# A decoder block on one core: the seventh product of a unit is put behind the next unit's first two

## The chip, the core and the metric

The kernel runs on one core of one Trainium2 chip. Five engines work side by side, each on its own queue in order: TensorE (PE in the profile; its weight loads are PEld), VectorE (DVE), ScalarE (ACT), GpSimd (POOL) and SyncE (SP), which here issues all DMA transfers. The metric is device time in microseconds, the median of the runs shown.

## The reference

One decoder layer over 2048 positions of width 1024, in float32. The input is normalised (RMSNorm) and projected once; the columns feed two mixers side by side. Their outputs are joined, projected, and added to the input; then comes a SwiGLU FFN of inner width 2816 with a residual, and a last RMSNorm.

```python
h = rmsnorm(x, norm1_g[l])
proj = h @ w_in[l]
p_q, p_k, p_v, p_g, p_a, c_b, c_c, c_h = jnp.split(proj, splits, axis=-1)
...
o = gla_chunked(q, k, v, log_a)          # 4 heads, 64 keys, 128 values, chunks of 64
o = rmsnorm(o, gla_norm_g[l]) * jax.nn.silu(p_g)
u = c_c * c_h
o_conv = c_b * causal_depthwise_conv(u, conv_w[l])   # width 3
mixed = jnp.concatenate([o_gla, o_conv], axis=-1) @ w_out[l]
x = x + mixed
h2 = rmsnorm(x, norm2_g[l])
ffn = (jax.nn.silu(h2 @ w_ffn_gate[l]) * (h2 @ w_ffn_up[l])) @ w_ffn_down[l]
x = x + ffn
return rmsnorm(x, norm_f_g)
```

## The kernel before

**Units of seven products.** The activations lie transposed, in blocks of 512 positions; the kernel works through them in two halves of two blocks each. The large products are done as 2 by 2 blocks: a unit (`unit`, L452) makes a 2 by 2 result, quarters (r, j) with r a block of 128 columns of the weights and j one of the half's two position blocks, by seven products instead of eight, in Strassen's manner (Winograd's form). `PRODUCTS` (L36) names the seven pairs of a weight quarter or a combination of quarters (A11, S1, S2, A12, S3, S4, A22) and an operand (B11, T1, T2, B21, T3, B22, T4). `unit_weights` (L424) loads the four quarters as one block `raw` (two buffers), makes S1 to S4 on POOL in place (S1 in a tile `s1` of its own) and splits each of the seven into a high and a low part (`split`, L162: one ACT instruction, then one DVE instruction), into tiles `wq` with four buffers. `product_step` (L443) adds high by high, high by low and low by high: three matmuls of 128 x 512 for each of the n blocks of 128 rows. n is 4 in the mixer's input projection and in FFN up, so a product has 12 matmuls; in the FFN's down projection it is 2 for the first group of inner blocks and 3 for the three others, 6 and 9 matmuls.

**Banks.** The eight PSUM banks come from one pool. A unit takes three: `oa` for the first, third, fifth and seventh product, `ob` for the second and sixth, and a third one for the fourth. Between two products in one bank the first has to be taken out: `copied` (ACT copy at L480, or, where the result is added to a running sum, `plus` on DVE at L473), and `plus` after the fourth, fifth and sixth product. The seventh is left in its bank, and whoever called `unit` takes it from there (`settled`, `silu`) or has it copied.

```python
oa = mul(0)
c11 = copied("c11", oa, (0, 0))
ob = mul(1)
c22 = copied("c22", ob, (1, 1))
mul(2, oa)
c12 = copied("c12", oa, (0, 1))
plus(c11, mul(3))
mul(4, oa)
plus(c22, oa)
mul(5, ob)
plus(c12, ob)
mul(6, oa)
```

**Stages.** `in_proj` (L749) runs twelve units for each half: keys and queries, values, the output gate, and for the convolution two rounds of three factors. Behind every second product `tick` (L241) takes one step of background work, among it the linear attention (`gla_half`), which `in_proj` starts after its sixth unit. Then `out_proj` (L935) without Strassen; for each half `ffn_up` (L1048), eleven pairs of a gate and an up unit, whose results go to DRAM split (`split_later`), and `ffn_down` (L1083), four groups of inner blocks (`GROUPS`) with four units each that add into tiles `y`. The last unit of all, `last_unit`, uses plain products with the final norm between them. The operands of a half or a group are loaded by `load_pairs`, `load_h2` or `group_op` into 28 tiles `op`; some (`WHOLE`) come unsplit and are split behind their load.

**Order.** The kernel is recorded in program order, and a scheduler of the tile layer then orders the instructions of each engine by its own model of time, so that a product's matmuls can stand interleaved with those of others. Marks (`issue_after`, `behind`) hold single instructions behind others.

Of the kernel before, what the change touches and what calls it, by code (L numbers as in the profile page):

```python
# [10 lines left out]
F32 = mybir.dt.float32  # L11
# [26 lines left out]
    ("S3", "T3"), ("S4", "B22"), ("A22", "T4"),  # L38
# [3 lines left out]
LATER = ("B21", "T3", "B22", "T4")  # L42
# [10 lines left out]
def tile_hymba_block(ctx, tc, x, xt, win, wa, wgu, wout, wffn, wdown, wdown_first, small, out):  # L53
# [370 lines left out]
    def unit_weights(src, raw=None):  # L424
# [7 lines left out]
        pool.tensor_tensor(a11, s1, a11, ALU.subtract)  # L432
# [4 lines left out]
        pool.tensor_tensor(a12, a12, a11, ALU.subtract)  # L437
# [14 lines left out]
    def unit(src, ops, into=None, onto=None, raw=None):  # L452
# [3 lines left out]
        w = unit_weights(src, raw)  # L456
# [25 lines left out]


# [178 lines left out]
    def load_pairs(src):  # L662
        ops = no_operands()
        for _, n in PRODUCTS:
            ops[n] = [(load_whole if n in WHOLE else load_pair)(p) for p in src[n]]
        return ops

# [81 lines left out]
    def in_proj(half, ops, first=None, differences=None):  # L749
        def units():  # L750
            for u in range(12):
                with ExitStack() as stack:
                    if half == 0 and u == 1:
                        stack.enter_context(tc.issue_after(last_load[0].ins))
                    if half or u > 1:
                        us = unit(win[u], ops)
                    else:
                        us = plain_unit(win[u], ops, differences) if u else first
                if half == 0 and u == 1:
                    del ops["B12"]  # L760
                    differences(("T4",))
                yield us

        units = units()
        for dst, i0 in ((s_kq, 0), (s_kq, 2), (s_v, 0), (s_v, 2)):
            for r, j, c, p in next(units):
                store(dst[2 * half + j][i0 + r][:], settled(c, p)[:])
        for i0 in (0, 2):
            for r, j, c, p in next(units):
                store(s_g[2 * half + j][i0 + r][:], silu(c, p)[:])  # L770
        background.append(gla_half(half))
        for i0 in (0, 2):
            cc = {(r, j): settled(c, p) for r, j, c, p in next(units)}
            ch = {(r, j): c for r, j, c, _ in next(units)}
            for r in range(2):
                i = i0 + r
                left = halo[:, i, :]
                for j in range(2):
                    s = tp.tile([P, PB + 2], F32, name="u", tag="t")
                    dve.tensor_tensor(s[:, 2:], ch[r, j][:], cc[r, j][:], ALU.mult)  # L780
                    act.activation(s[:, 0:2], left, AF.Copy)
                    left = s[:, PB : PB + 2]
                    y = cc[r, j]
                    act.activation(y[:], s[:, 0:PB], AF.Copy, scale=col(C_CW + i))
                    for n in (1, 2):
                        dve.scalar_tensor_tensor(
                            y[:], s[:, n : n + PB], col(C_CW + 4 * n + i), y[:], ALU.mult, ALU.add
                        )
                if half == 0:
                    act.activation(halo[:, i, :], left, AF.Copy)  # L790
            for r, j, c, _ in next(units):
# [7 lines left out]


# [238 lines left out]
    def load_h2():  # L1039
        ops, loads = no_operands(), raw_loads[-2]  # L1040
        for _, n in PRODUCTS:
            for k in range(4):
                with tc.issue_after(loads.ins):
                    o = (load_whole if n in WHOLE else load_pair)(s_h2p[n][k])
                ops[n].append(o)
        return ops

    def ffn_up(half, ops):  # L1048
        for m in range(NF // 2):
            us = unit(wffn[2 * m], ops)  # L1050
            sg = {(r, j): silu(c, p) for r, j, c, p in us}
            for r, j, c, _ in unit(wffn[2 * m + 1], ops):
                s = sg[r, j]
                dve.tensor_tensor(s[:], c[:], s[:], ALU.mult)
            b11, b12, b21, b22 = [sg[r, j] for r in range(2) for j in range(2)]
            t1, t2, t3, t4 = [bt(n) for n in ("t1", "t2", "t3", "t4")]
            for y, p, q in ((t1, b12, b11), (t2, b22, t1), (t3, b22, b12), (t4, b21, t2)):
                pool.tensor_tensor(y[:], p[:], q[:], ALU.subtract)
            values = [("B11", b11), ("B21", b21), ("B22", b22)]
            if half == 1 and m >= LAST_GROUP:  # L1060
                values.append(("B12", b12))
            values += [("T1", t1), ("T2", t2), ("T3", t3), ("T4", t4)]
            background.insert(0, split_later(s_act[half][m], values))
# [18 lines left out]

    def ffn_down(half):  # L1083
# [6 lines left out]
        for u, m0 in enumerate(GROUPS):  # L1090
# [4 lines left out]
            raw = None  # L1095
            if u:
                raw = raw_weights(wdown[4 * u - 4])
                with tc.issue_after(raw_loads[-1].ins):
                    ops = {n: [group_op(m, n) for m in ms] for _, n in PRODUCTS}
            else:  # L1100
                ops = {n: [group_op(m, n) for m in ms] for _, n in PRODUCTS}
# [5 lines left out]
            for d0 in range(0, KD, 2):  # L1107
# [6 lines left out]
                if u == 0:  # L1114
# [5 lines left out]
                    unit(src, ops, {(r, j): y[d0 + r, j] for r in range(2) for j in range(2)})  # L1120
                    continue
                xs = []
                if u < 3:
                    for d in (d0, d0 + 1):
                        xs.append((y[d, u - 1], bt("x1")))
                        load(xs[-1][1][:], s_x1[2 * half + u - 1][d][:])
# [4 lines left out]
                unit(src, ops, onto=onto, raw=None if d0 else raw)  # L1131
                for r, j in ((0, 0), (1, 1), (0, 1), (1, 0)):
# [6 lines left out]
                for yy, x1 in xs:  # L1139
                    pool.tensor_tensor(yy, x1[:], yy, ALU.add)  # L1140
# [247 lines left out]
```

## Time and profile before

| | |
|---|---|
| three runs | 2064.69, 2060.92, 2064.87 us |
| median | 2064.69 us |
| profiled execution: its span, first to last instruction | 2059.3 us |
| TensorE's share of the span | 98% |
| matmuls of `product_step` (three lines) | 3 x 2499 |
| DMA traffic | 421.47 MB, mean 205 GB/s |

No other time than its span is given for the profiled execution; the span leaves out what lies before the first and behind the last instruction. The page shows the busy share of each engine, the granted clock, the chain of work that ended last, and groups of equal instructions with their idle time and who ended it. The stages that its timeline shows are: the mixer's input projection to about 570 us, the output projection to about 760, then for each half FFN up and down, with the first half's down projection from about 1180 to 1410 and the second's from about 1820 on.

A row of the groups reads: line, engine, operation, output<-inputs, shape and count, then busy time, mean nanoseconds, and the idle time just before these instructions with its releasers. A row of the waits reads: engine, tile and line, <- who released it, then total us, number of times, the longest. A row of the timeline reads: start, duration, engine, line, operation, and in brackets the idle time before it.

### The profile page before, as it was taken

Reading aid. Unit: us, or ns where it says so; the run is one execution under the profiler, and the core shown is the slowest. Engines: PE = TensorE matmul, PEld = TensorE weight load, DVE = VectorE, ACT = ScalarE, POOL = GpSimd, SP = SyncE. Lnnn points to the kernel's source line nnn. Section 1 sums busy time; section 2 is a strip of 40 time slices with the busy share of each in tenths; the row PEclk is TensorE's granted clock in tenths of the full one; section 3 lists DMA queues with packets and bytes.
Section 4 is the critical chain, followed back from the end, with each engine's and each line's share of the span. In section 5 each row is a group of like instructions: output and inputs, shape, how many; then the busy total and the mean of one; then the engine's idle time right before and its main releaser. Section 6 shows DMA issues by size and latency. Waiting matters only on the chain.

```text
span 2059.3 us, 27063 instructions
## 1 busy us (share of the span) xinstructions
PE 2018.4 (98%) x9229; PEld 1657.3 (80%) x9229; DVE 1425.3 (69%) x2128; ACT 959.7 (47%) x1918; POOL 859.8 (42%) x622
## 2 busy tenths in 40 slices
PE   7999999999999999999999999999999999999997
PEld 6877888787888888888888878787888888878786
DVE  8789686559743886676675676767666666667774
ACT  6655365765542344444444452334434444453344
POOL 0345322122102564464564345534644544435544
PEclk9999999999999999999999999999999999999998
DMA  6378485416586873545454676476444434586653
GB/s 229 116 274 278 159 319 165 143 67 194 190 296 246 311 254 130 198 181 207 156 185 143 241 264 254 185 282 257 163 164 167 175 140 169 179 309 223 234 217 126
DMA packets 188729, 421.47 MB, mean 205 GB/s; under 512 B 19792, under 2 KB 65072, under 8 KB 178992
## 3 DMA queue, kind: packets, MB, share of 16 engines
q1 hardware_dynamic: 188592, 419.76, 57.2%
q8 instruction: 72, 1.18, 0.2%
q14 instruction: 65, 0.53, 0.1%
HBM read 274.98 MB, written 144.70 MB: 204 GB/s over the span
## 4 chain that ended last, share of the span: by engine, by line
PE 84%; DVE 7%; DMA 4%; ACT 3%; issue 1%; POOL 1%; SPq 0%; DVEq 0%; ACTq 0%; POOLq 0%
PE mm L448 24%; PE mm L449 23%; PE mm L450 23%; PE mm L945 3%; PE mm L948 3%; PE mm L946 3%; DVE wq L164 2%; DVE op L164 1%; DMA op<-sa_B 1%; DMA op<-sa_T 1%; PE a_ps L702 1%; ACT wq L163 1%; DMA siT<-lo 1%; PE o_ps L869 1%; PE o_ps L871 1%
## 5 line engine op out<-in xcount | busy, mean ns | idle before, releaser
L448 PE MATMUL mm<-op,wq 128*128 128x512 f32 x2499 | 973.7, 392 | 10.3 <-ACT c L480 5.3
L449 PE MATMUL mm<-op,wq 128*128 128x512 f32 x2499 | 972.5, 390 | 1.6 <-DVE op L164 1.6
L450 PE MATMUL mm<-op,wq 128*128 128x512 f32 x2499 | 961.3, 390 | 2.6 <-DVE wq L164 2.3
L164 DVE TENSOR_TENSOR wq<-raw,wq 128x512 fp32r<-128x512 f32 (+2 forms) x626 | 508.9, 818 | 262.6 <-ACT wq L163 260.0
L163 ACT ACTIVATE wq<-raw 128x512 fp32r<-128x512 f32 (+2 forms) x626 | 364.9, 589 | 585.6 <-PE mm L450 447.9
L448 PEld LDWEIGHTS mm<-op,wq 128*128 128x128 f32 x2499 | 468.9, 188 | 114.9 <-ACT c L480 8.0
L450 PEld LDWEIGHTS mm<-op,wq 128*128 128x128 f32 x2499 | 469.1, 188 | 103.8 <-DVE wq L164 6.1
L449 PEld LDWEIGHTS mm<-op,wq 128*128 128x128 f32 x2499 | 469.3, 188 | 99.1 <-DVE op L164 3.7
L432 POOL TENSOR_TENSOR raw<-s,raw 128x512 f32<-128x512 f32 (+2 forms) x97 | 133.3, 1374 | 518.5 <-DVE wq L164 474.7
L430 POOL TENSOR_TENSOR s<-raw 128x512 f32<-128x512 f32 (+2 forms) x97 | 127.4, 1313 | 247.5 <-DMA raw<-in_wffn_dram 90.7
L473 DVE TENSOR_TENSOR c<-mm,c 128x512 f32<-128x512 f32 x198 | 135.8, 686 | 72.7 <-PE mm L450 70.9
L473 DVE TENSOR_TENSOR y<-mm,y 128x512 f32<-128x512 f32 x185 | 126.9, 687 | 83.3 <-PE mm L450 82.9
L437 POOL TENSOR_TENSOR raw<-raw 128x512 f32<-128x512 f32 (+2 forms) x97 | 120.6, 1244 | 126.7 <-DVE wq L164 126.7
L927 POOL TENSOR_TENSOR ssx<-ssx,q 128x512 f32<-128x512 f32 x52 | 77.4, 1504 | 158.8 <-ACT q L926 158.5
L431 POOL TENSOR_TENSOR raw<-raw 128x512 f32<-128x512 f32 (+2 forms) x97 | 137.3, 1416 | 4.9
L480 ACT ACTIVATE c<-mm 128x512 f32<-128x512 f32 x198 | 116.1, 587 | 11.1 <-PE mm L450 9.3
L945 PE MATMUL mm<-op,wq 128*128 128x512 f32 x256 | 100.9, 395 | 0.0
L946 PE MATMUL mm<-op,wq 128*128 128x512 f32 x256 | 99.7, 389 | 0.0
L163 ACT ACTIVATE wq<-s 128x512 fp32r<-128x512 f32 (+2 forms) x97 | 56.9, 587 | 89.3 <-PE mm L450 85.4
L164 DVE TENSOR_TENSOR wq<-s,wq 128x512 fp32r<-128x512 f32 (+2 forms) x97 | 82.6, 852 | 2.8 <-ACT wq L163 2.1
L164 DVE TENSOR_TENSOR op<-op 128x512 fp32r<-128x512 f32 x94 | 76.8, 844 | 4.7 <-ACT op L163 4.6
L948 PE MATMUL mm<-op,wq 128*128 128x512 f32 x256 | 79.8, 390 | 0.0
(204 smaller groups left out, 1807.6 us busy)
## 6 DMA issues: line engine op xcount, KB each, us to landing
raw<-in_wffn_dram SPq DMA_DIRECT2D x44, 1024.0 KB, 6.5
sa_B<-so SPq DMA_DIRECT2D x47, 512.0 KB, 4.2
op<-sa_B SPq DMA_DIRECT2D x47, 512.0 KB, 7.1
raw<-in_win_dram SPq DMA_DIRECT2D x23, 1024.0 KB, 5.4
sa_T<-so SPq DMA_DIRECT2D x44, 512.0 KB, 4.5
op<-sa_T SPq DMA_DIRECT2D x44, 512.0 KB, 6.9
raw<-in_wdown_dram SPq DMA_DIRECT2D x24, 768.0 KB, 5.8
sx<-y SPq DMA_DIRECT2D x48, 256.0 KB, 4.0
```

Source lines behind the costliest of these rows:

```text
L163: last_hi[:] = [act.activation(hi, src, AF.Copy)]
L164: last_lo[:] = [dve.tensor_tensor(lo, src, hi.bitcast(F32), ALU.subtract)]
L430: pool.tensor_tensor(s1, a21, a22, ALU.add)
L431: pool.tensor_tensor(a21, a11, a21, ALU.subtract)
L432: pool.tensor_tensor(a11, s1, a11, ALU.subtract)
L448: pe.matmul(o[:], wh, xh, start=first and k == 0, stop=False, skip_group_check=True)
L449: pe.matmul(o[:], wh, xl, start=False, stop=False, skip_group_check=True)
L450: return pe.matmul(o[:], wl, xh, start=False, stop=k == n - 1, skip_group_check=True)
L473: dve.tensor_tensor(t[:], o[:], t[:], ALU.add)
L945: pe.matmul(o[e, j][:], wh, m[:, 0, :], start=k == 0, stop=False)
L946: pe.matmul(o[e, j][:], wh, m[:, 1, :], start=False, stop=False)
L948: pe.matmul(o[e, j][:], wl, ops[k][j][:, 0, :], start=False, stop=k == KD - 1)
```

## The change

The fifth and the sixth product change places: S4 by B22 comes before S3 by T3. S4 goes into `ob`, S3 into `oa`. A unit no longer ends with its seventh product: that becomes a generator `rest`, kept in `pending`, and the next `unit` runs it. `unit_weights` is a generator too and gives its splits in three portions: A11 and S1; S2, A12, S4 and S3; A22. A unit takes its first portion, then lets the previous unit split its A22, then takes its second portion. After its first two products it runs the previous unit's seventh. So `oa` is used for the first, third, sixth and seventh product of a unit, with two others between each, the last two of them products of the next unit.

Since a unit's last quarter comes later, the callers hand `unit` a function `use` that is called for each quarter, with the first three at the unit's end and (1, 0) behind the seventh product. `in_proj`, `ffn_up` and `ffn_down` are rewritten for this; the convolution runs for each r as soon as its two quarters are there, and FFN up makes T1 to T3 before the last quarter and T4 after it. The operand T4 of a new half or group is loaded late (`late`), after the old unit's seventh product, which still reads the old T4. With `close` a unit runs its own seventh product at once, with the fifth and sixth in the old order: the last unit of the input projection's second half and the one before `last_unit`.

```diff
 PRODUCTS = [
     ("A11", "B11"), ("S1", "T1"), ("S2", "T2"), ("A12", "B21"),
-    ("S3", "T3"), ("S4", "B22"), ("A22", "T4"),
+    ("S4", "B22"), ("S3", "T3"), ("A22", "T4"),
 ]
...
+    pending, late = [], []
+
+    def unit_weights(src, raw, w):
         raw = raw_weights(src) if raw is None else raw
...
-        w = {"A11": weight_quarter(a11)}
+        w["A11"] = weight_quarter(a11)
         pool.tensor_tensor(s1, a21, a22, ALU.add)
         pool.tensor_tensor(a21, a11, a21, ALU.subtract)
         pool.tensor_tensor(a11, s1, a11, ALU.subtract)
         w["S1"] = weight_quarter(s1)
+        halves.clear()
+        yield
         w["S2"] = weight_quarter(a11)
         w["A12"] = weight_quarter(a12)
-        w["S3"] = weight_quarter(a21)
         pool.tensor_tensor(a12, a12, a11, ALU.subtract)
         w["S4"] = weight_quarter(a12)
+        w["S3"] = weight_quarter(a21)
+        halves.clear()
+        yield
         w["A22"] = weight_quarter(a22)
         halves.clear()
-        return w
+        yield
...
+    def unit(src, ops, use=None, into=None, onto=None, raw=None, close=False):
+        w = {}
+        weights = unit_weights(src, raw, w)
+        next(weights)
+        before = pending.pop() if pending else iter(())
+        next(before, None)
+        next(weights)
...
+        def rest():
+            next(weights)
+            yield
+            mul(6, oa)
+            if into is not None or onto is not None:
+                copied("c21", oa, (1, 0))
+            if use is not None:
+                use(1, 0, oa, True)
+            yield
...
         ob = mul(1)
         c22 = copied("c22", ob, (1, 1))
+        next(before, None)
+        while late:
+            late.pop(0)()
         mul(2, oa)
         c12 = copied("c12", oa, (0, 1))
         plus(c11, mul(3))
-        mul(4, oa)
-        plus(c22, oa)
-        mul(5, ob)
+        if close:
+            mul(5, oa)
+            plus(c22, oa)
+        mul(4, ob)
         plus(c12, ob)
-        mul(6, oa)
-        if into is not None or onto is not None:
-            copied("c21", oa, (1, 0))
-        return [(0, 0, c11, False), (1, 1, c22, False), (0, 1, c12, False), (1, 0, oa, True)]
+        if not close:
+            mul(5, oa)
+            plus(c22, oa)
+        if use is not None:
+            for r, j, c in ((0, 0, c11), (1, 1, c22), (0, 1, c12)):
+                use(r, j, c, False)
+        pending.append(rest())
+        if close:
+            finish_unit()
...
+    def fill_now_or_late(n, fill):
+        if n == PRODUCTS[-1][1] and pending:
+            late.append(fill)
+        else:
+            fill()
...
+    def group_ops(ms, group_op, marks):
+        ops = no_operands()
+        for _, n in PRODUCTS:
+            def fill(n=n):
+                with behind(marks):
+                    ops[n] += [group_op(m, n) for m in ms]
+            fill_now_or_late(n, fill)
+        return ops
```

More of the change, by code (lines that the diff above doesn't have):

```diff
@@ L764, in in_proj, with run @@
[L764 to L767, printed above, removed]
+        count = iter(range(12))
+        def run(use):
+            u = next(count)
+            if half or u > 1:
+                unit(win[u], ops, use, close=half == 1 and u == 11)
+                return
+            us = first
+            if u:
+                with tc.issue_after(last_load[0].ins):
+                    us = plain_unit(win[u], ops, differences)
+                del ops["B12"]
+                differences(("T4",))
+            for x in us:
+                use(*x)
@@ L1130, in ffn_down, with use @@
                 onto = {(r, j): y[d0 + r, j] for r in range(2) for j in range(2)}
[L1131 to L1132 removed]
+                def use(r, j, *_, onto=onto, xs=xs, last=last, d0=d0):
                     yy = onto[r, j]
```

153 lines of the change are left out of this document (82 added, 71 removed).

## The prediction

> **What bounds the kernel now.** I read the page first (share of each engine, clock, chain), then the groups by line on TensorE, then the waits of TensorE by stage, and last the timeline around single stalls.
>
> ```profile
> span 2059.3 us, 27063 instructions
> PE 2018.4 (98%) x9229; PEld 1657.3 (80%) x9229; DVE 1425.3 (69%) x2128; ACT 959.7 (47%) x1918; POOL 859.8 (42%) x622
> PEclk9999999999999999999999999999999999999998
> PE 84%; DVE 7%; DMA 4%; ACT 3%; issue 1%; POOL 1%; SPq 0%; DVEq 0%; ACTq 0%; POOLq 0%
> ```
>
> TensorE is busy 98% of 2059.3 us at full clock, and the chain that ended last is 84% TensorE. No operation is added or removed by this change, so only TensorE's stalls can move. How many there are, by the groups:
>
> ```profile
> L448 PE MATMUL mm<-op,wq 128*128 128x512 f32 x2499 | 973.7, 392 | 10.3 <-ACT c L480 5.3 <-DVE y L473 3.4 <-DVE c L473 1.4
> L449 PE MATMUL mm<-op,wq 128*128 128x512 f32 x2499 | 972.5, 390 | 1.6 <-DVE op L164 1.6
> L450 PE MATMUL mm<-op,wq 128*128 128x512 f32 x2499 | 961.3, 390 | 2.6 <-DVE wq L164 2.3
> ```
>
> The three lines of product_step idle for 10.3 + 1.6 + 2.6 = 14.5 us. The 10.3 us in front of L448 are banks: a product may not start in a bank until ACT (L480) or DVE (L473) has taken the previous one out. The 2.3 us are weights split late, the 1.6 us operands split late. What one stall costs, start to start:
>
> ```profile
> 159.25 0.39 PE L449 MATMUL mm<-op,wq 128*128 128x512 f32 x1
> 159.47 0.39 PE L450 MATMUL mm<-op,wq 128*128 128x512 f32 x1
> 161.59 0.50 PE L448 MATMUL mm<-op,wq 128*128 128x512 f32 x1 [1.72 <-ACT c L480]
> 161.92 0.40 PE L449 MATMUL mm<-op,wq 128*128 128x512 f32 x1
> 162.16 0.40 PE L450 MATMUL mm<-op,wq 128*128 128x512 f32 x1
> ```
>
> Undisturbed matmuls follow each other by 0.22 to 0.23 us (0.227 below). Here 2.12 pass, so 1.89 us are lost, and 0.33 instead of 0.23 behind it another 0.10: a stall costs its idle time plus 0.27 us. The waits of TensorE in 30 to 450 us (first half of the mixer), in 815 to 1190, in 1190 to 1440, and in 1440 to 1830 us, one fence each:
>
> ```profile
> PE mm L450 <- DVE wq L164: 1.8, 4, 0.6
> PE mm L448 <- ACT c L480: 1.7, 1, 1.7
> PE mm L448 <- DVE c L473: 0.7, 1, 0.7
> ```
>
> ```profile
> PE mm L448 <- ACT c L480: 1.2, 1, 1.2
> ```
>
> ```profile
> PE mm L448 <- ACT c L480: 1.7, 1, 1.7
> PE mm L448 <- DVE y L473: 1.7, 2, 1.5
> PE mm L449 <- DVE op L164: 1.6, 2, 1.4
> PE mm L450 <- DVE wq L164: 0.3, 1, 0.3
> ```
>
> ```profile
> PE mm L448 <- ACT c L480: 0.7, 1, 0.7
> PE mm L448 <- DVE c L473: 0.4, 1, 0.4
> ```
>
> The stalls are few and single: four waits for ACT's copy make up its whole 5.3 us (1.7, 1.2, 1.7, 0.7). Why such a copy is late, at the second of them:
>
> ```profile
> 831.47 1.29 POOL L316 TENSOR_TENSOR t<-h,t 128x512 f32<-128x512 f32 x1 [1.47 <-DVE so L164]
> 831.91 1.40 DVE L164 TENSOR_TENSOR wq<-raw,wq 128x512 fp32r<-128x512 f32 x1
> 833.24 0.68 DVE L1054 TENSOR_TENSOR c<-c,c 128x512 f32<-128x512 f32 x1
> 833.95 0.63 ACT L163 ACTIVATE so<-c 128x512 fp32r<-128x512 f32 x1 [2.76 <-DVE c L1054]
> 834.49 0.58 ACT L480 ACTIVATE c<-mm 128x512 f32<-128x512 f32 x1
> 835.12 0.50 PE L448 MATMUL mm<-op,wq 128*128 128x512 f32 x1 [1.18 <-ACT c L480]
> ```
>
> ACT's copy takes 0.58 us, but stands in ACT's queue behind a split (so<-c) that waits for DVE, which is held up by a weight split of 1.40 us that runs beside a POOL instruction. So the evacuation is on time or late by other people's work, and what counts is how many matmuls lie between.
>
> **The change, part by part.** I counted distances in the order of both built programs: from the last matmul on which the awaited instruction depends, through its engine's queue too, to the matmul that waits. One matmul is 0.227 us.
>
> First finding: the scheduler has already mixed the units. In the built kernel before, in FFN up, most units run A11, eleven matmuls of S1, the previous unit's A22, the last of S1, A12, S2, S4, S3. That is the changed program order but for one matmul and A12. So TensorE's order hardly moves there; what moves are distances:
>
> ```
> median distance, matmuls           before   after
> bank before S2, mixer first half       22      26   (lowest quarter 13 -> 25)
> bank before S3, mixer first half       12      26
> bank before S3, FFN up, halves 1, 2  17.5, 23   23, 23
> weights of A11 and S1, same stages  24-26   35-38
> bank before A22, down projection       18      16
> raw block: load may go to first use
>   FFN up / down / first group   121/89/76   97/64/67 (lowest 82/61/73 -> 64/52/43)
> ```
>
> 1. S2 and S3 rest longer (the swap of S3 and S4, and A22 put between). Of the four ACT stalls, three go from 13, 0 and 5 matmuls to 16 or more: a gain of at least 3 matmuls = 0.7 us for the first bound, typically 10 to 16 = 2.3 to 3.6 us, against lateness of 1.7, 1.7 and 0.7. I take all three as gone: 4.1 idle. The one at 835 us goes from 12 only to 14, so 0.45 of its 1.2 goes. Two small ones (at 200.94 and 773.73 us, under the bound at which a wait is listed) I leave out. Gain 4.6 idle, three restarts at 0.27 = 0.8: 5.4 us. Bounds: 0 (ACT is late by another 2 us) to 6.4.
>
> 2. Weights are split earlier by about ten matmuls, since each wq buffer waits for the product four places ahead and that is now less often at a unit's end. Ten matmuls are 2.3 us and the four waits before 450 us were 0.6 at most: all gone, 1.8 + 4 x 0.27 = 2.9 us. Bounds 0 and 2.9. The wait at 1687 us, where A22's distance goes from 2 to over 16, goes too: 0.4 + 0.27 = 0.7.
>
> 3. A22 behind the next unit's first two products. In the mixer its distance stays at 22 to 24, and in down projection it falls from 18 to 16. Its stalls, which I keep:
>
> ```profile
> 391.99 0.50 PE L448 MATMUL mm<-op,wq 128*128 128x512 f32 x1 [0.67 <-DVE c L473]
> 1197.38 0.50 PE L448 MATMUL mm<-op,wq 128*128 128x512 f32 x1 [1.53 <-DVE y L473]
> ```
>
> Two matmuls less are 0.45 us. About 32 waits have this distance and two in the whole run were late (3.4 us in the first table's L473 y, with S3's), so I add 0.5. Bounds 0 and 32 x 0.45 = 14.
>
> 4. New tight places. In the first units of FFN up (where position_rstd takes banks beside them) the built program puts A22 twice directly behind the S3 of its own bank: distance 0. The price of one is between DVE's bare add and the stall at 1427 us, which also had distance 0:
>
> ```profile
> L473 DVE TENSOR_TENSOR c<-mm,c 128x512 f32<-128x512 f32 x198 | 135.8, 686 | 72.7 <-PE mm L450 70.9
> 1427.72 0.50 PE L448 MATMUL mm<-op,wq 128*128 128x512 f32 x1 [1.70 <-ACT c L480]
> ```
>
> Between 0.7 and 1.7 + 0.27 = 2.0; the middle, 1.3, twice: 2.6 us. In each half's first down group one S4 has distance 6 = 1.4 us behind ACT's copy of 0.58: 0.3 each, bounds 0 and 1.0 (the 0.7 stall at distance 5): 0.6 us.
>
> 5. Held longer: the raw block (two buffers) is freed only when A22's quarter is split, so the next block's load starts later, and what stands behind it in SP's queue too. With A22 move its split (one on ACT, one on DVE), its bank's eviction, and the (1, 0) quarter's consumer with its store on SP, which now comes behind the loads for the next unit; nothing on TensorE waits for these stores soon, except sa_ blocks at the first down group. What the load needs, 1208 to 1440 us:
>
> ```profile
> L145 SPq DMA_DIRECT2D raw<-in_wdown_dram x12: 328/333/582, 1208.2 to 1362.7; - x12
> DMA to landing us min/median/max: 4.1/6.2/11.1
> L163 ACT ACTIVATE wq<-raw 128x384 fp32r<-128x384 f32 x142 | 73.7, 525 | 170.0 <-PE mm L450 138.6 <-POOL raw L437 20.7 <-POOL raw L432 10.2
> L164 DVE TENSOR_TENSOR wq<-raw,wq 128x384 fp32r<-128x384 f32 x142 | 96.2, 679 | 11.7 <-ACT wq L163 11.7
> ```
>
> 64 matmuls are 14.5 us; landing 6.2 and a split of 0.5 + 0.7 are 7.4, the longest 11.1 makes 12.3. The worst place has 52 = 11.8 us. Normal loads are hidden by seven us of products; I cost nothing. Without that cover each us of delay costs 1 us in each of 32 units.
>
> 6. The rest is costed at nothing. The late fill of T4 (the last operand) gives its four loads more room behind the old unit's A22. Consumers by quarter (use) issue the same ACT, DVE and POOL instructions. GLA's background starts two products later, with six units to run in. [...] The prologue up to 30 us and last_unit keep their order.
>
> Sum: -5.4 - 2.9 - 0.7 + 0.5 + 2.6 + 0.6 = -5.3 us, so 2054.0 us on the profiled span. The span is 5.4 us (0.26%) under the median of the runs shown, 2064.7, within which that execution's edges lie; I take the difference over: 2064.7 - 5.3 = 2059.4 us.
>
> [...]
>
> **The rivals.**
>
> Nothing moves: the scheduler had done the change's work already, as its order in FFN up shows, and what was late by queues (the 1.40 us split) is late at another place, so that the 5.4 + 2.9 + 0.7 us of points 1 and 2 come back at about the size of points 3 and 4: 2064.7, give or take 4. For it: the stalls are single ones of 0.3 to 1.7 us, spread over four stages. Against: the distances do grow, and of the waits of product_step in the run before none with a distance above 30 stalled.
>
> Slower: the later raw blocks (point 5). It decides when landing passes 14.5 - 1.2 = 13.3 us in down projection, twice the median, as when SP's queue holds the load behind a store that waits. One unit in two late by 1 us gives 16 us: 2059.4 + 16 = 2075. Against: the longest landing was 11.1.
>
> More than forecast: down projection's stalls vanish as well. All of the 14.5 idle and the restarts of the 15 waits listed above, at 0.27, are 18.6 us: 2046. If half of what points 1 to 3 leave goes, it is about 2053.
>
> **How the numbers follow.** Forecast (own range 2055 to 2064) 0.5; nothing moves 0.17; slower 0.18; more 0.15. Faster by over 0.2% means under 2060.6, about what a measurement of this kernel can tell from no change (the three runs lie 0.19% apart): 0.40 of the forecast's 0.5 and the 0.15 give 0.55. Within 0.2%: 0.1 and 0.12, so 0.22. Slower: 0.18 and 0.05, so 0.23. The range reaches to 2049, half way into the gain beyond, and to 2071, past half way to the slower case.
>
> **What would show it.** In the changed profile: L480 in front of product_step's first matmul under 2 us in total (was 5.3) shows point 1; no wait for wq before 450 us shows point 2; two waits for DVE c of 0.7 to 2 us between 780 and 830 us show point 4; POOL's L430 form or ACT's split waiting for raw by DMA, and then TensorE waiting for wq after 1190 us, would show point 5 wrong. The prediction is wrong if new waits on L473 in down projection add up to more than 5 us, or if the operand waits of 1.4 us at the group changes multiply.

## The result and the profile after

The changed kernel takes 2074.64 us in the median (2074.32 to 2079.58, five runs), against 2062.89 us for the kernel before in runs beside it (2060.92 to 2064.87, five runs). The ratio is 1.0067, with a 95% interval of 1.0055 to 1.008: it is slower by 0.67%. The forecast was 2059.4 with a range from 2049 to 2071, so the time lies outside the range and on the other side.

The page of the changed kernel: span, busy shares, granted clock in 40 slices, and the chain that ended last.

```profile
span 2072.9 us, 27199 instructions
PE 2025.9 (98%) x9229; PEld 1661.7 (80%) x9229; DVE 1410.1 (68%) x2128; ACT 967.5 (47%) x1918; POOL 835.8 (40%) x622
PEclk9999999999999999999999999999999999999999
PE 89%; DVE 4%; DMA 3%; ACT 2%; issue 1%; POOL 1%; SPq 0%; DVEq 0%; ACTq 0%; POOLq 0%
```

Again 9229 matmuls and a TensorE that is busy for 98%, but the span is 13.6 us longer. The page alone does not say where. The groups of product_step (lines 454 to 456 are the former 448 to 450):

```profile
L454 PE MATMUL mm<-op,wq 128*128 128x512 f32 x2499 | 974.9, 393 | 16.3 <-ACT c L848 5.4 <-DVE osb L953 3.2 <-ACT wq L163 3.0
L455 PE MATMUL mm<-op,wq 128*128 128x512 f32 x2499 | 974.9, 390 | 0.1
L456 PE MATMUL mm<-op,wq 128*128 128x512 f32 x2499 | 969.2, 391 | 7.0 <-DVE wq L164 6.5
```

Idle time rises from 14.5 to 23.4 us. The busy time of the three lines rises as well, by 11.5 us (974.9 + 974.9 + 969.2 against 973.7 + 972.5 + 961.3), with the same matmuls: some of them ran slower, and a longer idle time is not the whole loss. The waits of TensorE, as total, times and longest, are now few and large:

```profile
PE mm L456 <- DVE wq L164: 6.5, 6, 2.5
PE mm L454 <- ACT c L848: 5.4, 1, 5.4
PE mm L454 <- DVE osb L953: 3.2, 1, 3.2
PE mm L454 <- ACT wq L163: 3.0, 5, 1.3
PE mm L454 <- DVE y L484: 2.6, 4, 0.9
PE mm L454 <- DVE rs L217: 1.8, 2, 0.9
```

ACT's copies out of the banks (5.3 us before, L480, now L491) have no row any more. In their place stand three single stalls in the mixer, at 146, 411 and 479 us, of 2.5, 3.2 and 5.4 us.

**The stall at 411 us** begins with a raw block. Some lines of each engine in turn, from the timeline of the changed kernel:

```profile
393.54 0.37 SPq L145 DMA_DIRECT2D raw<-in_win_dram  x1
400.11 1.28 POOL L432 TENSOR_TENSOR s<-raw 128x512 f32<-128x512 f32 x1 [14.23 <-DMA raw<-in_win_dram]
401.34 1.29 POOL L440 TENSOR_TENSOR raw<-raw 128x512 f32<-128x512 f32 x1
402.67 0.63 ACT L163 ACTIVATE wq<-raw 128x512 fp32r<-128x512 f32 x1 [4.02 <-POOL raw L440]
403.21 0.26 ACT L948 ACTIVATE sq<-o_ps 128x128 f32<-128x128 f32 x1
409.89 0.69 DVE L953 TENSOR_TENSOR osb<-o_ps,hsq 128x512 f32<-128x512 f32 x1
410.72 0.47 PE L454 MATMUL mm<-op,wq 128*128 128x512 f32 x1 [3.20 <-DVE osb L953]
```

The block is asked for at 393.54 and landed when POOL, idle for 14.23 us, begins at 400.11. ACT had nothing late of its own, but its next instruction was the split of a quarter that POOL had not made, so ACT stood for 4.02 us, and behind it in its queue the attention's sum of squares (L948). That work is what DVE needs before it can take the attention's output out of its bank (L953), and TensorE's next product wanted that bank. The last of the attention's own matmuls (L926) had started at 399.42, so L948 could have begun some 3 us earlier; from there to L953 it went its usual way, with two table loads of 1.28 us on ACT in it. The quarter that ACT waited for is not even one of the late block: `unit_weights` makes L432, L433, L434, L440 in this order, so the L440 that stands between the L432 and the L433 of the late block belongs to the block before it and had been held up in POOL's queue behind that L432. The weights were late, but what stopped TensorE was not the weights: it was the queues that waited for them.

**The stall at 479 us** has no late block. The DVE queue and the stalled matmul:

```profile
474.47 0.69 DVE L484 TENSOR_TENSOR c<-mm,c 128x512 f32<-128x512 f32 x1
475.07 0.68 DVE L164 TENSOR_TENSOR wq<-raw,wq 128x512 fp32r<-128x512 f32 x1
475.67 0.69 DVE L785 TENSOR_TENSOR g<-g 128x512 f32<-128x512 f32 x1
476.27 0.75 DVE L775 TENSOR_SCALAR g<-z,sml 128x512 f32<-128x512 f32 x1
476.94 0.74 DVE L850 SCALAR_TENSOR_TENSOR c<-u,sml,c 128x512 f32<-128x512 f32 x1
477.59 0.69 DVE L844 TENSOR_TENSOR u<-c,c 128x512 f32<-128x512 f32 x1
478.20 0.69 DVE L484 TENSOR_TENSOR c<-mm,c 128x512 f32<-128x512 f32 x1
479.03 0.76 PE L454 MATMUL mm<-op,wq 128*128 128x512 f32 x1 [5.38 <-ACT c L848]
```

Between two evacuations (L484) DVE works off a weight split (L164), the second half's forget gate (L775 to L787) and the first half's convolution (L844, L850) without a gap. The row names ACT's L848 as releaser, but by the kernel's text that instruction touches no bank; the one that reads a bank here is L484, which ended at 478.89, 0.14 us before the matmul.

**Half clock.** After such stalls the matmuls come at 0.43 us instead of 0.23. The trace's clock records have four stretches at 0.5 between start and end, 3.4, 3.4, 6.8 and 3.4 us long, at the stalls of 146, 411, 479 and 1427 us (the last one, in the FFN, idles for 1.26 and then 0.29 us); the kernel before had none. In the table of windows of the changed kernel (us, busy time of the five engines with counts, granted clock, DMA share, GB/s):

```profile
137.00:143.00 6.00, 5.88 (x27) 4.55 (x25) 3.32 (x5) 2.45 (x5) 4.86 (x4) 1.00 0.72 246
143.00:149.00 6.00, 3.49 (x9) 2.48 (x8) 6.00 (x7) 2.25 (x6) 3.94 (x4) 0.72 0.98 339
```

Counted over the gaps between the starts of neighbouring matmuls, from the 200th to the 9229th: the excess over 0.227 us in gaps of more than 0.45 us went from 24.7 to 32.5 us, that in gaps of 0.40 to 0.45 us (the half clock) from 1.3 to 7.0, and all the rest fell by 0.8. That is 7.8 + 5.7 - 0.8 = 12.7 us; 1.1 us more lie ahead of the 200th matmul, and 0.1 less behind the last. So two fifths of the loss are no wait at all, but the slow matmuls behind the waits.

### The profile page after: what moved, and what is told of

Its sections match the earlier page's. It is cut to its first block, busy times and chain, and to the rows that moved or that the text cites. A ratio compares the mean times of both kernels' runs of the same rounds, so it can differ in the third digit from the quotient of the medians.

```text
span 2072.9 us, 27199 instructions
## 1 busy us (share of the span) xinstructions
PE 2025.9 (98%) x9229; PEld 1661.7 (80%) x9229; DVE 1410.1 (68%) x2128; ACT 967.5 (47%) x1918; POOL 835.8 (40%) x622
## 4 chain that ended last, share of the span: by engine, by line
PE 89%; DVE 4%; DMA 3%; ACT 2%; issue 1%; POOL 1%; SPq 0%; DVEq 0%; ACTq 0%; POOLq 0%
PE mm L454 25%; PE mm L456 25%; PE mm L455 25%; PE mm L1000 3%; PE mm L1001 3%; PE mm L1003 3%; DVE op L164 1%; DMA op<-sa_B 1%; DVE wq L164 1%; PE a_ps L743 1%; DMA raw<-in_win_dram 1%; PE o_ps L924 1%; PE o_ps L926 1%; DMA raw<-in_wdown_first_dram 1%; DVE y L484 0%
## 5 line engine op out<-in xcount | busy, mean ns | idle before, releaser
L454 PE MATMUL mm<-op,wq 128*128 128x512 f32 x2499 | 974.9, 393 | 16.3 <-ACT c L848 5.4
L456 PE MATMUL mm<-op,wq 128*128 128x512 f32 x2499 | 969.2, 391 | 7.0 <-DVE wq L164 6.5
L455 PE MATMUL mm<-op,wq 128*128 128x512 f32 x2499 | 974.9, 390 | 0.1
L164 DVE TENSOR_TENSOR wq<-raw,wq 128x512 fp32r<-128x512 f32 (+2 forms) x626 | 497.4, 800 | 358.1 <-ACT wq L163 356.0
L163 ACT ACTIVATE wq<-raw 128x512 fp32r<-128x512 f32 (+2 forms) x626 | 360.4, 586 | 508.1 <-PE mm L456 301.1
L454 PEld LDWEIGHTS mm<-op,wq 128*128 128x128 f32 x2499 | 471.0, 188 | 122.4 <-ACT wq L163 13.3
L456 PEld LDWEIGHTS mm<-op,wq 128*128 128x128 f32 x2499 | 470.6, 188 | 110.5 <-DVE wq L164 12.2
L432 POOL TENSOR_TENSOR s<-raw 128x512 f32<-128x512 f32 (+2 forms) x97 | 119.6, 1233 | 419.1 <-DMA raw<-in_win_dram 125.2
L434 POOL TENSOR_TENSOR raw<-s,raw 128x512 f32<-128x512 f32 (+2 forms) x97 | 130.1, 1341 | 276.1 <-DVE wq L164 267.3
L440 POOL TENSOR_TENSOR raw<-raw 128x512 f32<-128x512 f32 (+2 forms) x97 | 116.9, 1205 | 175.8 <-DVE wq L164 165.8
L484 DVE TENSOR_TENSOR y<-mm,y 128x512 f32<-128x512 f32 x185 | 126.5, 686 | 70.3 <-PE mm L456 69.7
L484 DVE TENSOR_TENSOR c<-mm,c 128x512 f32<-128x512 f32 x198 | 135.6, 685 | 55.1 <-PE mm L456 54.8
L491 ACT ACTIVATE c<-mm 128x512 f32<-128x512 f32 x198 | 115.6, 588 | 118.1 <-PE mm L456 116.4
L433 POOL TENSOR_TENSOR raw<-raw 128x512 f32<-128x512 f32 (+2 forms) x97 | 130.3, 1343 | 4.5
L1117 POOL TENSOR_TENSOR t<-c,c 128x512 f32<-128x512 f32 x44 | 66.9, 1520 | 84.3 <-DVE c L1121 79.3
L1000 PE MATMUL mm<-op,wq 128*128 128x512 f32 x256 | 100.7, 395 | 0.0
L1001 PE MATMUL mm<-op,wq 128*128 128x512 f32 x256 | 99.8, 390 | 0.0
L164 DVE TENSOR_TENSOR wq<-s,wq 128x512 fp32r<-128x512 f32 (+2 forms) x97 | 96.1, 990 | 1.6 <-ACT wq L163 1.2
L164 DVE TENSOR_TENSOR op<-op 128x512 fp32r<-128x512 f32 x94 | 76.5, 844 | 6.5 <-ACT op L163 6.5
```

What stands on the lines that cost most here:

```text
L163: last_hi[:] = [act.activation(hi, src, AF.Copy)]
L164: last_lo[:] = [dve.tensor_tensor(lo, src, hi.bitcast(F32), ALU.subtract)]
L454: pe.matmul(o[:], wh, xh, start=first and k == 0, stop=False, skip_group_check=True)
L455: pe.matmul(o[:], wh, xl, start=False, stop=False, skip_group_check=True)
L456: return pe.matmul(o[:], wl, xh, start=False, stop=k == n - 1, skip_group_check=True)
L484: dve.tensor_tensor(t[:], o[:], t[:], ALU.add)
```

## The experiments

The raw blocks come later, as POOL's waits for them show, before and after:

```profile
POOL s L430 <- DMA raw<-in_wffn_dram: 90.7, 22, 6.9
POOL s L430 <- DMA raw<-in_win_dram: 27.2, 7, 9.1
POOL s L430 <- DMA raw<-in_wdown_dram: 12.6, 11, 2.3
```

```profile
POOL s L432 <- DMA raw<-in_win_dram: 125.2, 18, 14.2
POOL s L432 <- DMA raw<-in_wffn_dram: 123.5, 21, 10.2
POOL s L432 <- DMA raw<-in_wdown_dram: 60.3, 19, 6.8
```

In the mixer POOL waited seven times and now 18 times. My theory was that this is the loss: A22's quarter is split two products later, so the block's buffer is free later. The rival was that queues run over by chance of order, whatever the blocks do (crowding). The first four kernels were to part them. Throughout, each time is the median, beside the kernel before on the same chip (2062.94, 2061.85, 2062.44 and 2061.84 us for the four groups of runs).

**Half of the change each.** `ffn_only` closes all units of the input projection, `mix_only` all units of the FFN.

```diff
-                unit(win[u], ops, use, close=half == 1 and u == 11)
+                unit(win[u], ops, use, close=True)
```

```diff
-        unit(wffn[2 * m], ops, gated)
-        unit(wffn[2 * m + 1], ops, raised)
+        unit(wffn[2 * m], ops, gated, close=True)
+        unit(wffn[2 * m + 1], ops, raised, close=True)
...
-                close = bool(last and half and d0 == KD - 4)
+                close = True
```

> The changed kernel, but every unit of the mixer's input projection runs its own seventh product at once (close), with the fifth and sixth product in the old order; the FFN overlaps as changed. Crowding theory (in the mixer the fourth quarter's consumers and the convolution come two products later and meet the background's work on DVE and ACT): the stalls of 2.7, 3.4 and 5.5 us at 146, 411 and 479 us and the half-clock matmuls behind the last two go; about 10 us of the 11.8 come back, 2064 to 2067 us against 2062.9 before. Late-block theory (the raw block is freed later everywhere, in the FFN as in the mixer): also faster, but the FFN's stalls at 1197, 1427, 1857 us stay, so 2066 to 2069. If the loss were spread evenly over the units: 48 of 166 overlapping units are undone, 2071.

> The changed kernel with the overlap only in the mixer's input projection; every unit of FFN up and down closes. Crowding theory: nearly the whole loss stays, 2072 to 2075 us. Late-block theory, even over stages: about a third to a half of the loss stays, 2067 to 2070.

Measured: 2072.22 us (ratio 1.005, 1.0038 to 1.0063) and 2078.9 us (1.0081, 1.0067 to 1.0095). Both are slow, so the two do not add up, and the expectations for both failed: both theories wanted the first under 2070 and the second no slower than 2075 (for the first, a loss spread evenly, 2071, came nearest). They were not the clean halves that I took them for: a closed unit runs S3 before S4, as before, but `unit_weights` still splits S4's weights ahead of S3's. TensorE's waits for weights in `mix_only` fit that, 10.3 us where the kernel before had 2.3:

```profile
PE mm L456 <- DVE wq L164: 10.3, 12, 2.5
```

By the profiled executions the closed stages lose as well: in `ffn_only` the mixer to the end of the output projection takes 9.6 us longer than before, and in `mix_only` what follows takes 7.0 us longer. And in the closed mixer of `ffn_only` the blocks came early (POOL's wait, then TensorE's longest between 60 and 560 us):

```profile
POOL s L432 <- DMA raw<-in_win_dram: 7.7, 3, 2.9
```

```profile
PE sc L900 <- DVE kq L890: 4.8, 1, 4.8
```

This stall ends at 483 us, with DVE again busy without a gap with the forget gate and the convolution. So the crowd near 480 us needs neither the overlap nor a late block. These two runs say that a loss does not need the overlap, not where all of it comes from. What `mix_only` does show is that a stall is a property of the order: with the mixer's part unchanged, its stalls of 3.1 and 5.4 us, for L953 and L848, are there again.

**A22's quarter apart.** In `a22_apart` the quarter has a tile of its own with three buffers, so the rest of the block is free at S3's split; it comes by three transfers. The tiles for ten instead of eleven `b` buffers pay for the space, and `bx10` is the changed kernel with those ten buffers alone.

```diff
-        raw = rawp.tile([P, 4 * PB], F32, name="raw", tag="raw")[:, 0 : 4 * n]
-        raw = raw.rearrange("p (a n) -> p a n", a=4)
-        raw_loads.append(load(raw, src))
-        return raw
+        raw = rawp.tile([P, 3, PB], F32, name="raw", tag="raw")[:, :, 0:n]
+        a22 = rawp.tile([P, PB], F32, name="a22", tag="a22", bufs=3)[:, 0:n]
+        load(raw[:, 0:2, :], src[:, 0:2, :])
+        load(raw[:, 2, :], src[:, 3, :])
+        raw_loads.append(load(a22, src[:, 2, :]))
+        return [raw[:, 0, :], raw[:, 1, :], a22, raw[:, 2, :]]
```

> The changed kernel with the quarter A22 loaded into a tile of its own with three buffers (three DMAs a block instead of one), so the other three quarters' two buffers are free before A22 is split; to make room the pools bx and fx have 10 buffers instead of 11. Late-block theory: POOL's waits for the raw block by DMA (125 us for win, 123 for wffn) fall under 60 in all, the stalls at 411 and 1427 us go, and 6 to 10 us come back, 2065 to 2069. Crowding theory: the stall of 5.5 us at 479 us stays, and less than 4 us come back, 2071 to 2075.

> The changed kernel with 10 buffers instead of 11 in the pools bx and fx alone: the price of the room that the kernel with A22 apart needs. Both theories: within 3 us of the changed kernel, 2072 to 2078; it is the one that the kernel with A22 apart has to be compared with.

Measured: 2064.47 us (1.001, 1.0001 to 1.0019) and 2075.1 us (1.0064, 1.0052 to 1.0077). The tile gives back 10.6 us. In its trace the waits of POOL for blocks and of TensorE are:

```profile
POOL s L434 <- DMA raw<-in_win_dram: 71.3, 9, 32.3
POOL s L434 <- DMA raw<-in_wffn_dram: 36.0, 9, 10.2
```

```profile
PE mm L456 <- ACT c L852: 5.1, 1, 5.1
PE mm L458 <- DVE wq L164: 4.7, 6, 1.4
```

The stalls at 146 and 411 us are gone (the longest wait for weights is 1.4 instead of 2.5, and L953 has no row), and so is the one at 1427 us. The 5.1 us at the old 479 us stay. POOL's waits for the blocks of the mixer and of FFN up fell to 107.3 us, from 244.3 in `bx10`, not under 60 as expected, and one new stall of 2.25 us came at 197.74 us. The tile shifts every queue, so the time alone would not prove the cause; with the chain at 411 us and the stalls that went with the waits, late blocks are one cause, and there is a second.

**Only one part of the change.** `swap_only` is the kernel before with S3 and S4 exchanged everywhere; `overlap_only` is the changed kernel with S3 and S4 in their old order.

```diff
...
-    ("S3", "T3"), ("S4", "B22"), ("A22", "T4"),
+    ("S4", "B22"), ("S3", "T3"), ("A22", "T4"),
...
-        w["S3"] = weight_quarter(a21)
         pool.tensor_tensor(a12, a12, a11, ALU.subtract)
         w["S4"] = weight_quarter(a12)
+        w["S3"] = weight_quarter(a21)
...
-        mul(4, oa)
-        plus(c22, oa)
-        mul(5, ob)
+        mul(4, ob)
         plus(c12, ob)
+        mul(5, oa)
+        plus(c22, oa)
         mul(6, oa)
```

> The kernel before with only S3 and S4 exchanged: in the order of products, of their operands and of their weight splits. A22 stays in its own unit, so no raw block is held longer. In the two halves of the overlap that ran so far, the mixer cost the same 8 to 9 us more than before whether its units overlapped or were closed, and what the closed one still had of the change is the splits' new order. Late-block theory: 2061 to 2065, as before, with at most 30 us of waits of the first weight subtraction for blocks of the mixer. Exchange theory (S4's weights now stand ahead of S3's on POOL, ACT and DVE, and the DVE queue near 480 us runs over): 2068 to 2073, with a stall of 4 to 6 us between 470 and 495 us.

> The changed kernel with S3 and S4 in the order of before (products, operands and weight splits), A22 still behind the next unit's first two products. Late-block theory: the block is held as long as in the changed kernel, so 2072 to 2077, with over 100 us of waits of the first weight subtraction for blocks of the mixer and a half-clock stretch behind a stall of 3 us or more. Exchange theory: 2063 to 2067.

Measured: 2069.73 us (1.0038, 1.0026 to 1.0051) and 2070.13 us (1.0042, 1.003 to 1.0055). Neither theory has both: the late blocks do not explain the first, and the second lies between the two expectations, with 111.8 us of waits for blocks in the mixer and three half-clock stretches, as the late-block theory wanted. The exchange alone costs 7.9 us with the blocks' waits in the FFN as before (90.1 us, 22 times), and without the stall of 4 to 6 us that the exchange theory wanted; its loss is many small ones:

```profile
L448 PE MATMUL mm<-op,wq 128*128 128x512 f32 x2499 | 975.1, 393 | 14.6 <-ACT c L480 7.4 <-DVE c L473 3.8 <-DVE y L473 2.9
L450 PE MATMUL mm<-op,wq 128*128 128x512 f32 x2499 | 963.4, 391 | 7.4 <-DVE wq L164 7.2
```

Waits for weights grow from 2.3 to 7.2 us and those for evacuations from 10.3 to 14.6. What makes these late one by one I have not traced to an end; so no cause is shown for the 7.9 us that the exchange alone costs.

**The early gate.** `gate_early` puts the second half's forget gate at the front of the background work. Its scans on DVE (L781) then stand at 302 to 316 us instead of 455 to 484.

```diff
-    background.append(gate(1, ops))
+    background.insert(0, gate(1, ops))
```

> The changed kernel with the second half's forget gate put at the front of the background work instead of behind the first half's attention, so that its DVE work is done before the convolution of the first half begins. Crowding theory: the stall at 479 us (5.5 us and 2.3 us of half clock behind it) goes or falls under 2 us, 2067 to 2070. Late-block theory alone: this stall too is a late block, and stays: 2073 to 2076.

Measured: 2061.89 us (1.0001, 0.9992 to 1.001), 12.7 us less than the changed kernel and more than expected. Its eleven runs spread from 2059.97 to 2067.54, and the profiled execution is the slowest of them, so what its trace shows is the bad case. Blocks came as late as ever, and still of the three large stalls in the mixer only the one at 146 us is left (POOL's waits, then TensorE's from 60 to 560 us); a new one of 1.8 us at 363 us has a half-clock stretch with it:

```profile
POOL s L432 <- DMA raw<-in_win_dram: 146.6, 18, 13.2
```

```profile
PE mm L456 <- DVE wq L164: 2.5, 1, 2.5
PE mm L454 <- ACT c L538: 1.8, 1, 1.8
```

This corrects the first theory: what a late block costs TensorE depends on what stands in the queues behind it. With 146.6 us of waiting for blocks the stall at 146 us is left, without half clock behind it, and the one at 411 us is not there; with 125.2 us in the changed kernel both stood. The early gate also moves the attention's steps, which come behind it in the background, and that is likely how the stall at 411 us went along; it was not tried apart.

**Both aids, with and without the change.** `apart_gate` is the changed kernel with both aids; `before_apart`, `before_gate` and `before_both` are the kernel before with the tile (and its ten buffers), the early gate, and both; `overlap_both` is `overlap_only` with both. Their edits are the ones shown.

> The changed kernel with both aids: A22's quarter in its own tile (three buffers, ten b buffers) and the second half's forget gate at the front of the background work. Each alone gave back 10 to 12 us. If they mend different stalls (late blocks everywhere; DVE's crowding near 479 us), they add: 2050 to 2055, faster than both kernels. If they mend the same two stalls of the mixer (411 and 479 us), only the FFN's 4.7 us that the tile gave comes on top of the early gate: 2055 to 2060. If every new order draws its own stalls, it lies with the other variants: 2062 to 2070.

> The kernel before with A22's quarter of each raw block in a tile of its own (three buffers) and ten instead of eleven b buffers: the same aid that gave the changed kernel 10.6 us. Late-block theory: the kernel before has few late blocks (27 us of waits in the mixer, seven times), so the aid gives it nothing: 2061 to 2065. If the aid works by something else (three transfers instead of one, other places in memory), the kernel before gains by it too: 2053 to 2059.

> The kernel before with the second half's forget gate at the front of the background work. Crowding theory: the kernel before has only 1.45 us of excess at this place (in front of a scores matmul at 476 us), so there is little to gain: 2060 to 2063. If the early gate is good by itself, as it gave the changed kernel 12 us: 2050 to 2055. If every new order draws its own stalls: 2066 to 2071, as with the other variants of this kernel.

> The kernel before with both aids (A22's quarter in a tile of its own, early gate) and nothing of the change: what the change is worth once its late blocks and the crowded place near 479 us are out of the way is the difference between this kernel and the changed one with both aids (2054.1). If the overlap itself gains what the prediction's points 1 and 2 put on it (5.4 and 2.9 us, or 8.3 with 0.7 more less 3.7 of costs): 2059 to 2063. If the aids do it all and the overlap nothing: 2052 to 2056. If the tile harms the kernel before in the mixer and the FFN by the 8 us it did alone: 2065 to 2069.

> The changed kernel with both aids, but S3 and S4 in the order of before. If the exchange is worth something (S2's bank rests for two products instead of one before S3): 2057 to 2064. If A22's move alone does the work: 2052 to 2056.

| kernel | median us | ratio to before | interval | matmuls 200 to 3588, us | 3588 to 9229, us | half-clock stretches |
|---|---|---|---|---|---|---|
| before | 2062.89 | 1 | | 703.3 | 1290.0 | 0 |
| changed | 2074.64 | 1.0067 | 1.0055 to 1.008 | 712.5 | 1293.5 | 4 |
| changed, tile | 2064.47 | 1.001 | 1.0001 to 1.0019 | 707.8 | 1288.8 | 2 |
| changed, early gate | 2061.89 | 1.0001 | 0.9992 to 1.001 | 705.5 | 1294.0 | 1 |
| changed, both | 2054.12 | 0.996 | 0.9946 to 0.9974 | 698.7 | 1288.2 | 0 |
| before, tile | 2070.28 | 1.0036 | 1.0023 to 1.0048 | 710.1 | 1291.5 | 3 |
| before, early gate | 2059.24 | 0.9985 | 0.9976 to 0.9994 | 701.6 | 1288.9 | 1 |
| before, both | 2063.24 | 1.0004 | 0.9995 to 1.0013 | 701.8 | 1292.8 | 1 |
| overlap alone, both | 2065.33 | 1.0014 | 1.0005 to 1.0023 | 707.7 | 1283.1 | 2 |

Each ratio is to the kernel before in the runs of its own group. The two stage columns are from each profiled execution: the time from the 200th to the 3588th matmul, the last of the output projection in every one of these kernels, and from there to the last. The last column counts stretches at clock 0.5 between start and end. The profiled execution of `overlap_both` was the fastest of its eleven (2060.60 us), so its stages flatter it; those of the changed kernel with the early gate and with both, and of the kernel before with the tile, were the slowest of theirs.

Of the five expectations, the first came true (2050 to 2055) and two were missed by a hair: the early gate in the kernel before (2059.24, expected from 2060) and both aids in it (2063.24, expected to 2063). The tile in the kernel before (2070.28) and `overlap_both` (2065.33) lie outside everything that was expected of them.

The aids nearly add up in the changed kernel: 10.2 and 12.7 us alone, 20.5 together. With both it is the fastest of all, 0.40% under the kernel before. And with both, the change is worth what it was made for: 2063.24 without it, 2054.12 with it, 9.1 us. Part of that is the harm that the tile does to the kernel before; against the best kernel without the change, the one with the early gate alone (2059.24), it is 5.1 us. The groups of the two show which of the prediction's terms that is, first the kernel before with both aids (L450 is the first matmul of a step, L452 the third), then the changed one (L456, L458):

```profile
L450 PE MATMUL mm<-op,wq 128*128 128x512 f32 x2499 | 973.0, 392 | 9.7 <-ACT c L482 8.6 <-DVE c L475 0.4 <-ACT op L163 0.4
L452 PE MATMUL mm<-op,wq 128*128 128x512 f32 x2499 | 962.6, 390 | 2.6 <-DVE wq L164 2.6
```

```profile
L456 PE MATMUL mm<-op,wq 128*128 128x512 f32 x2499 | 971.9, 392 | 9.2 <-DVE c L486 2.8 <-DVE y L486 2.3 <-DVE rs L217 2.1
L458 PE MATMUL mm<-op,wq 128*128 128x512 f32 x2499 | 967.1, 390 | 4.6 <-DVE wq L164 4.6
```

ACT's copies held TensorE for 8.6 us without the change, and with it they are not among the first three (1.5 us); waits for weights do not fall but rise, from 2.6 to 4.6. `overlap_both` does not gain, so A22's move does not pay without the exchange; whether the exchange pays without A22's move is open, as it was not run with both aids. The kernel before gains nothing from the tile, it loses 8.4 us by it, which shows that the tile is no aid by itself. Why it loses there is open: it has half-clock stretches at 144, 605 and 1424 us that the kernel before had not, and POOL waited less for blocks than there (29.9 us instead of 90.7 in FFN up). So the sum of these waits does not rank the kernels, and a reordering by itself can cost as much as what is to be explained.

## Why the prediction was wrong, by its steps

**Point 1** (banks rest longer, -5.4) was right, in mechanism and about in size. The sign it named, L480's waits under 2 us, is there: from 5.3 us to no row, and with both aids from 8.6 to 1.5.

**Point 2** (weights split about ten matmuls earlier, -2.9) was wrong. By the prediction no wait for wq before 450 us would show it; there is one of 2.5 us at 145.89 us, and the total rose from 2.3 to 6.5 us. The ten matmuls were counted from TensorE's order to the free wq buffer; that the split itself can start was taken for granted. It waits for POOL, and POOL for the block, which for this stall was asked for at 130.4 us and had landed when POOL began at 138.14. POOL stood idle for only 1.34 us of that; operations for other work stood between its steps.

**Point 3** (A22 in down projection, +0.5) was harmless, as costed: the waits for y went from 3.4 us in three to 2.6 in four.

**Point 4** (two tight places, 1.3 each) was right. The stalls are at 807.66 and 829.23 us, each 1.04 us longer than the pace, though the row names DVE's rs L217 and not c. That they came near the middle of so wide a bracket (0.7 to 2.0) is luck.

**Point 5** (the raw block held longer, "I cost nothing") is the step that failed: a term put at nothing, of which A22's tile gave back 10.6 us (`a22_apart` against `bx10`), 4.5 of them in the mixer and 5.0 behind it by the profiled executions. How much of this is the blocks and how much the new order of the queues is not shown. The distances were counted in the built program and the landing time was right: it did not grow (median 5.4 and now 5.6 us in the mixer, 30 to 570 us). Wrong was the comparison of a typical landing with the cover on TensorE; already in the prediction's own numbers the longest landing with its split, 12.3 us, did not fit the worst place, 11.8. What has to lie within the cover is the queueing as well: the wait for SP's turn, POOL's operations of 1.3 us each, and then whatever stands behind the waiting split on ACT and DVE. And I worked it out for the down projection, where the distance was lowest, while most of the loss came in the mixer (9.2 us to the end of the output projection, 3.5 behind it), where at one place 14.23 us of POOL's wait met queues full of attention, gate and convolution. The rival "slower" had the right cause and by accident nearly the right time (2075), with the wrong place and the wrong threshold: no landing passed 13.3 us in any stall followed here.

**Point 6** (GLA's background and the consumers by quarter "cost nothing") failed too. Putting the gate elsewhere gave 12.7 us back, where the kernel before gained 3.2; so where background work lies against a stage whose evacuations share DVE is a term of the sum, and I named no cover for it.

**The price of a stall**, idle time plus 0.27 us, holds to about 0.2 us where the clock stays full, as at a stall of 3.06 us at 411.73 in `bx10` (3.33 us from start to start, where 0.23 is the pace). It fails where the half clock comes, which added 5.7 us in the sum, and which stalls bring it is not a matter of length alone (last section). It had been read from one stall of 1.72 us.

**The first rival** has what was late by queues come back at another place. Three edits that take a part or an aid alone (`swap_only`, `overlap_only`, `before_apart`) cost 0.36 to 0.42%. That they lose is measured; what decides where the lateness comes is not shown by any run here.

## What to carry to other kernels

When a buffer is held longer, follow the late transfer through every queue that it passes, not only to its own consumer: the engine that waits for it stops everything behind it, and TensorE may then wait for something that has nothing to do with the transfer. Here, at 411 us, POOL stood for 14.23 us and ACT for 4.02, and TensorE then waited 3.20 us for a bank with the attention's output. A change that removes the stalls it was meant to remove can still lose to where other work happens to lie; look at what shares the queue at the new stalls, move that, and measure the change again with it moved. And a stall can be dearer than its length: the one of 2.51 us at 146 us cost 1.4 us more than the one of 2.52 us in `bx10`, by the slow matmuls behind it.

## What was not expected of the hardware

Of two equal stalls one cost 1.4 us more than the other. The changed kernel and `bx10` have the same stall, 2.51 and 2.52 us for the same weights, one microsecond apart. First the changed kernel, then `bx10`: the matmul that stalled, and the seventh behind it.

```profile
145.89 0.79 PE L456 MATMUL mm<-op,wq 128*128 128x512 f32 x1 [2.51 <-DVE wq L164]
149.02 0.40 PE L454 MATMUL mm<-op,wq 128*128 128x512 f32 x1
```

```profile
144.94 0.51 PE L456 MATMUL mm<-op,wq 128*128 128x512 f32 x1 [2.52 <-DVE wq L164]
146.67 0.39 PE L454 MATMUL mm<-op,wq 128*128 128x512 f32 x1
```

```profile
143.00:149.00 6.00, 4.06 (x18) 3.36 (x19) 6.00 (x9) 2.23 (x5) 3.98 (x3) 1.00 0.99 349
```

Seven matmuls take 3.13 us in the one and 1.73 in the other, and the windows from 143 to 149 us show a granted clock of 0.72 there and 1.00 here (last row). `gate_early` has the stall too, 2.52 us at 145.00 us, and its seven matmuls take 1.72 us. A longer stall, of 3.06 us at 411.73 us in `bx10`, has a granted clock of 1.00 around it as well (409 to 415 us), while a shorter one, of 1.8 us at 363 us in `gate_early`, has a half-clock stretch with it (0.96 as the mean of 340 to 380 us). So the length of a stall alone does not tell whether slow matmuls follow; what does is not shown here.
